# A log-softmax backward kernel: sixteen straight passes become one straight pass and a staged loop

## Chip, cores and metric

One core of a Trainium2 chip. Kernels are compared only within the same rounds. Times are device microseconds (us). "A is x% slower" is computed as the mean time of one kernel's runs over that of the other's of the same rounds, so it is not quite the ratio of the medians that stand beside it.

## The reference

```python
# y, dy: [8, 1024, 8192] float32
softmax_x = np.exp(y)
sum_dy = np.sum(dy, axis=-1, keepdims=True)
out = dy - softmax_x * sum_dy
```

8192 rows of 8192 columns; each tensor is 268.4 MB, so 805.3 MB must move in any case.

## The kernel before

A group is 256 rows (128 partitions, two rows in each, a tile of 8.39 MB), and there are 32. A pass treats two: six tiles in seven transfers (dy, y, dy, y in two halves, two stores), all issued by SP. There is little room: two dy tiles, in which the result is built as well, and one y tile a little longer than a group, in which the second group's y begins to overwrite the first's. So what SP may issue depends on what VectorE has finished and which stores have landed.

```python
    def sums(x):                                   # negated row sums, one row on each engine
        nc.vector.tensor_reduce(out=s_t[:, 0:1], in_=x[:, :D], ..., op=ALU.add, negate=True)
        nc.scalar.activation(x[:, D:], x[:, D:], COPY, accum_out=second_t[:])
        nc.vector.tensor_scalar(out=s_t[:, 1:2], in0=second_t[:], scalar1=-1.0, ...)
    ...
    def compute(x, s_t, at, r, pieces):            # three pieces to a row
        for b, e in pieces:
            nc.scalar.activation(y_t[:, ys], y_t[:, ys], EXP)
            nc.vector.scalar_tensor_tensor(out=x[:, xs], in0=y_t[:, ys], scalar=s_t[:, r : r + 1],
                                           in1=x[:, xs], op0=ALU.mult, op1=ALU.add)

    for g in range(0, G, 2):                       # 16 passes, all unrolled
        load_dy(g, x_ts[0])
        load_y(g, SHIFT, 0, W)
        s_t = sums(x_ts[0])
        for r in range(R):
            compute(x_ts[0], s_t, SHIFT, r, PIECES_A)
        load_dy(g + 1, x_ts[1])
        s_t = sums(x_ts[1])
        for r in range(R):
            load_y(g + 1, 0, r * D, (r + 1) * D)
            compute(x_ts[1], s_t, 0, r, PIECES_B)
        for j in range(2):
            nc.sync.dma_start(out=out_v[g + j], in_=x_ts[j][:])
```

## Time and profile before

| | before |
|---|---|
| time, median (range) of 4 runs | 1866.73 us (1866.56 to 1866.97) |
| span of the profiled run | 1866.1 us |
| VectorE, ScalarE busy | 46%, 37% |
| DMA queue, share of 16 engines' span | 99.8%, 432 GB/s |

The prediction below shows the page, the chain and the timeline.

### The profile page before, as it was taken

Reading aid. Unit: us, or ns where it says so; the run is one execution under the profiler, and the core shown is the slowest. Engines: PE = TensorE matmul, PEld = TensorE weight load, DVE = VectorE, ACT = ScalarE, POOL = GpSimd, SP = SyncE. Lnnn points to the kernel's source line nnn. Section 1 sums busy time; section 2 is a strip of 40 time slices with the busy share of each in tenths; the row PEclk is TensorE's granted clock in tenths of the full one; section 3 lists DMA queues with packets and bytes.
Section 4 is the critical chain, followed back from the end, with each engine's and each line's share of the span. In section 5 each row is a group of like instructions: output and inputs, shape, how many; then the busy total and the mean of one; then the engine's idle time right before and its main releaser. Section 6 shows DMA issues by size and latency. Waiting matters only on the chain.

```text
span 1866.1 us, 843 instructions
## 1 busy us (share of the span) xinstructions
DVE 857.9 (46%) x256; ACT 689.3 (37%) x257; POOL 0.2 (0%) x4
## 2 busy tenths in 40 slices
DVE  2907429074290742807328073280732806338163
ACT  2606326063260532605326053260523605235152
POOL 0000000000000000000000000000000000000000
DMA  9999999999999999999999999999999999999998
GB/s 427 427 427 427 431 444 429 427 434 443 427 434 438 425 435 442 428 429 431 440 431 430 438 427 436 437 440 427 430 438 435 428 437 428 438 435 434 434 428 386
DMA packets 16134, 805.36 MB, mean 432 GB/s; under 512 B 1792, under 2 KB 1792, under 8 KB 1792
## 3 DMA queue, kind: packets, MB, share of 16 engines
q1 hardware_dynamic: 16128, 805.31, 99.8%
q14 instruction: 6, 0.05, 0.0%
HBM read 536.87 MB, written 268.44 MB: 432 GB/s over the span
## 4 chain that ended last, share of the span: by engine, by line
DMA 65%; DVE 14%; another core or an unknown queue 10%; ACT 9%; issue 0%; DVEq 0%; ACTq 0%; SPq 0%
DMA x<-in_dy_dram 31%; DMA out_dram<-x 30%; DVE x L74 14%; ACT x L60 6%; ACT y_t L73 3%; DMA y_t<-in_y_dram 3%; DVEq L121 0%; ACTq L121 0%; SPq L52 0%; ACTq L73 0%; ACTq L60 0%
## 5 line engine op out<-in xcount | busy, mean ns | idle before, releaser
L74 DVE SCALAR_TENSOR_TENSOR x<-y_t,s_t,x 128x1024 f32<-128x1024 f32 (+2 forms) x192 | 579.4, 3059 | 257.5 <-ACT y_t L73 257.5
L57 DVE TENSOR_REDUCE s_t<-x 128x1 f32<-128x8192 f32 x32 | 277.8, 8682 | 721.9 <-DMA x<-in_dy_dram 721.9
L73 ACT ACTIVATE y_t<-y_t 128x1024 f32<-128x1024 f32 (+2 forms) x192 | 460.1, 2466 | 280.0 <-DMA y_t<-in_y_dram 280.0
L60 ACT ACTIVATE x<-x 128x8192 f32<-128x8192 f32 x32 | 225.0, 7030 | 863.2 <-DMA x<-in_dy_dram 863.2
L60 ACT ACTIVATION_READ_ACCUMULATOR x<-x 128x1 f32 x32 | 6.0, 187 | 0.0
L61 DVE TENSOR_SCALAR s_t<-second_t 128x1 f32<-128x1 f32 x32 | 4.6, 143 | 0.0
L60 ACT ACT_TABLE_LOAD x1 | 1.3, 1283 | 0.7 <-PEq L110 0.7
L110 POOL MEMSET const-uint8-127<- 128x1 uint8 x1 | 0.1, 102 | 0.0
L110 POOL MEMSET const-bfloat16-1.0<- 128x1 bf16 x1 | 0.1, 101 | 0.0
L110 POOL MEMSET const-float32-0.0<- 128x1 f32 x1 | 0.1, 98 | 0.2 <-issue 0.2
L110 POOL MEMSET const-float32-1.0<- 128x1 f32 x1 | 0.1, 98 | 0.0
## 6 DMA issues: line engine op xcount, KB each, us to landing
y_t<-in_y_dram SPq DMA_DIRECT2D x32, 4096.0 KB, 22.1
x<-in_dy_dram SPq DMA_DIRECT2D x32, 48.4
out_dram<-x SPq DMA_DIRECT2D x32, 32.6
y_t<-in_y_dram SPq DMA_DIRECT2D x16, 57.5
```

What stands on the lines that cost most here:

```text
L57: nc.vector.tensor_reduce(out=s_t[:, 0:1], in_=x[:, :D], axis=mybir.AxisListType.X, op=ALU.add, negate=True)
L60: nc.scalar.activation(x[:, D:], x[:, D:], COPY, accum_out=second_t[:])
L61: nc.vector.tensor_scalar(out=s_t[:, 1:2], in0=second_t[:], scalar1=-1.0, scalar2=None, op0=ALU.mult)
L73: nc.scalar.activation(y_t[:, ys], y_t[:, ys], EXP)
L74: nc.vector.scalar_tensor_tensor(out=x[:, xs], in0=y_t[:, ys], scalar=s_t[:, r : r + 1], in1=x[:, xs], op0=ALU.mult, op1=ALU.add,)
L110: nc = _bacc.Bacc("TRN2", target_bir_lowering=False, num_devices=1)
```

## The change

The intent is a program a fraction as long that runs as fast. A loop must reset its semaphores in each round. A plain loop does so at a barrier. The staged ("staggered") loop cuts the body into four stages instead: an engine enters a stage only when all five have reported the stage before last as done. The reports default to late points, so the change places some by hand. It also states that the two stores don't depend on each other, since with a row number known only at run time the dependency analysis must assume that they may.

```diff
-    for g in range(0, G, 2):
-        load_dy(g, x_ts[0])
-        load_y(g, SHIFT, 0, W)
+    def done_early():
+        for engine in (mybir.EngineType.Activation, mybir.EngineType.DVE):
+            tc.previous_stage_wait(engine)
+
+    def two_groups(h, boundary, early):
+        load_dy(h, 0)
+        load_y(h, 0, SHIFT, 0, W)
+        boundary()
+        early()
         s_t = sums(x_ts[0])
         for r in range(R):
             compute(x_ts[0], s_t, SHIFT, r, PIECES_A)
-        load_dy(g + 1, x_ts[1])
+        load_dy(h, 1)
+        boundary()
+        early()
         s_t = sums(x_ts[1])
         for r in range(R):
-            load_y(g + 1, 0, r * D, (r + 1) * D)
+            load_y(h, 1, 0, r * D, (r + 1) * D)
             compute(x_ts[1], s_t, 0, r, PIECES_B)
-        for j in range(2):
-            nc.sync.dma_start(out=out_v[g + j], in_=x_ts[j][:])
+        boundary()
+        stores = [nc.sync.dma_start(out=out_v[h, j], in_=x_ts[j][:]) for j in range(2)]
+        tc.declare_no_dep(stores[1].ins, stores[0].ins, reason="different rows of out")
+
+    two_groups(0, lambda: None, lambda: None)
+    with tc.For_i(1, G // 2, 1, iteration_sync="staggered") as h:
+        two_groups(h, tc.stage_boundary, done_early)
```

Cut: the index of the group is split in two (`h`, `j`) in the views and helpers.

## The prediction

> **What bounds the kernel now.** I read the page first. Its opening lines carry the argument: no compute engine is busy for half of the span, and the DMA engines are busy in every slice.
>
> ```profile
> span 1866.1 us, 843 instructions
> DVE 857.9 (46%) x256; ACT 689.3 (37%) x257; POOL 0.2 (0%) x4
> DMA packets 16134, 805.36 MB, mean 432 GB/s; under 512 B 1792, under 2 KB 1792, under 8 KB 1792
> q1 hardware_dynamic: 16128, 805.31, 99.8%
> q14 instruction: 6, 0.05, 0.0%
> ```
>
> 805.31 MB is exactly two inputs and one output of 268.4 MB each, so no byte is moved twice, and the queue's packets fill 99.8% of the engines' time. The kernel can become faster only if the same bytes move at a higher rate, or slower only if the queue runs dry.
>
> Next, the chain that ended last, in order of time (start, length, what). I take it for the rhythm, not for its shares.
>
> ```profile
> 450.09 38.98 DMA x<-in_dy_dram
> 529.22 37.31 DMA out_dram<-x
> 566.55 38.78 DMA x<-in_dy_dram
> ...
> 1613.11 38.60 DMA x<-in_dy_dram
> 1729.17 38.60 DMA x<-in_dy_dram
> ```
>
> One pass over two groups takes 566.55 - 450.09 = 116.46 us, and late in the run 1729.17 - 1613.11 = 116.06. A pass moves six tiles of 8.39 MB; 116.06 / 6 = 19.34 us a tile, 434 GB/s. The best passes have no gap at all.
>
> Third, the timeline of one pass, to see how much work the queue holds whenever the issuing engine, SP, has to issue something (start, length, engine, line, operation).
>
> ```profile
> 489.10 8.69 DVE L57 TENSOR_REDUCE s_t<-x 128x1 f32<-128x8192 f32 x1 [46.92 <-DMA x<-in_dy_dram]
> 508.50 14.32 ACT L73 ACTIVATE y_t<-y_t 128x1024 f32<-128x1024 f32 x6 [12.22 <-DMA y_t<-in_y_dram]
> 512.46 16.73 DVE L74 SCALAR_TENSOR_TENSOR x<-y_t,s_t,x 128x3328 f32<-128x3328 f32 x5 [1.58 <-ACT y_t L73]
> 516.17 9.25 SPq L67 DMA_DIRECT2D y_t<-in_y_dram  x2
> 527.79 7.03 ACT L60 ACTIVATE x<-x 128x8192 f32<-128x8192 f32 x1 [4.96 <-DMA x<-in_dy_dram]
> 529.22 29.78 SPq L95 DMA_DIRECT2D out_dram<-x  x2
> 547.29 7.22 ACT L73 ACTIVATE y_t<-y_t 128x2048 f32<-128x2048 f32 x3 [2.55 <-DMA y_t<-in_y_dram]
> 551.89 6.75 DVE L74 SCALAR_TENSOR_TENSOR x<-y_t,s_t,x 128x3072 f32<-128x3072 f32 x2 [0.30 <-ACT y_t L73]
> 566.55 0.34 SPq L52 DMA_DIRECT2D x<-in_dy_dram  x1
> 566.99 0.77 SPq L67 DMA_DIRECT2D y_t<-in_y_dram  x1
> 585.84 0.33 SPq L52 DMA_DIRECT2D x<-in_dy_dram  x1
> ```
>
> What an engine was released by tells when a transfer landed: dy of the first group at 489.1, its y at 508.5, dy of the second at 527.8, the halves of its y at 537.5 and 547.3, the stores (each releases the load into its own buffer) at 566.5 and 585.8. Against this I set the issue times and get the reserve, the work still queued at an issue:
> - y halves: issued from 516.17; dy of the second group lasts until 527.8. Reserve 11.6 us.
> - first store: issued 529.22; the y halves last until 547.3. Reserve 18.1 us.
> - second store: VectorE ends at 551.89 + 6.75 = 558.64, and the issue follows at once; the first store lasts until 566.5. Reserve 7.9 us, the smallest of the pass.
> - next dy: issued 566.55, when the first store has landed; the second lasts until 585.8. Reserve 19.3 us.
> - second dy: issued 585.84; dy and y lie in the queue, 38.7 us.
> A delay on SP below its reserve costs nothing.
>
> **What the Trainium skill says.** "DMA: Bandwidth & Descriptors", section Specifications, gives a fabric ceiling of 435 GB/s and about 358 GB/s of HBM for one core. The trace agrees with the first (432 over the span, 434 in a clean pass) and not with the second. "Advanced Engine Details and Errata", section Control Flow Timing, puts an unconditional branch at about 51 ns and a compare-and-branch at about 108 ns; before has no loop, so its trace cannot say. "Runtime: NRT & Kernel Launch", section Instruction fetch mechanics, says that a taken branch to a page out of the window stalls for a fetch by DMA; before shows only straight fetching, the 6 packets above. The DMA page's section "Anatomy of one DMA" puts the fixed cost of a transfer near 2.0 us (for the other way of issuing). Here the first load is issued at 0.73 and first used at 22.47: 21.74 less 19.34 of data is 2.4 us. That is what an empty queue would cost each time, and I use 2.4.
>
> **The change part by part.** I compared the built programs engine by engine.
>
> *Removed:* 14 of 16 straight copies of a pass: one stays ahead of the loop, one becomes the body, run 15 times. Transfers, sizes, order and issuing queue stay, as do all compute instructions: 16 x 116.06 = 1857.0 us of data remains. SP's program falls from 98 rows to 28, VectorE's from 226 to 36. So most of the 6 instruction fetches should vanish. The ceiling of what this can give is the excess of the uneven passes: the 14 intervals between successive first loads, from 100.82 to 1729.17, sum to 1628.35 us, against 14 x 116.06 = 1624.84, so 3.5 us in all, of which the fetches are part. I put in -1 us.
>
> *Added, loop entry:* a barrier of all engines, once. VectorE ends the first pass near 92.9 (the first pass matches the one above), SP next needs to issue at 100.82. An estimate of 1 us fits into 7.9. Cost 0.
>
> *Added, stage handshakes:* four stages. Before each, SP counts down "my stage before last is done", waits until all five engines have, resets counters of another stage and reports itself in. That is 2 to 5 semaphore instructions a boundary; no row shows one of these, so I take an estimate of 0.1 us each, guided by the skill's branch figures: 0.2 to 0.5 us. I checked what each boundary waits for:
> - before the first store: all have finished the first group. Here the early report matters. ScalarE and VectorE report it at the start of the second group's work, after their own last piece of the first (VectorE near 529.2), not when the second group is done. The first store moves from 529.2 to at most 529.7, against 18.1 us. Cost 0.
> - before the next dy: the second group is done (558.64) and the back edge is taken. SP has some ten short instructions here, estimated 1.1 us: it is ready near 560, and must wait for the first store until 566.5 anyway. Cost 0.
> - before the second dy: both stores have landed. The load into that buffer waits for the second store anyway, and 38.7 us are queued. Cost 0.
> - before the y halves: the first group's loads have landed (508.5). The free buffer comes later, at 516.2. Cost 0.
> VectorE pays a handshake between its groups, 0.5 us estimated. Its reduction of 8.69 us then ends near 538.3, while the first piece starts at 539.47, since it waits for ScalarE: inside 1.2 us. The 7.9 us reserve at the second store is untouched.
>
> *Added, addresses:* one register instruction for each of 7 transfers, placed before the wait for data or followed by a queue that is full. 0.
>
> *Declared:* the second store need not wait for the first. In before it doesn't either (issue at 558.7, first landing at 566.5), and the built after waits for VectorE alone there. This keeps what was, and gains nothing.
>
> *End:* the barrier after the loop runs under the last store, about 27 us long (558.64 to 585.84 in the middle). Only GpSimd's second reset instruction comes after the landing, estimated at 0.4 us, with nothing to hide it.
>
> Sum: 1866.65 + 0 x 15 - 1.0 + 0.4 = 1866.05, so 1866.0 us.
>
> **The rivals.**
> 1. The stages serialize: the first store waits until the second group is computed. Then it goes out at 558.6 instead of 529.2, the queue is empty from 547.3 on, 11.3 + 2.4 = 13.7 us a pass, x 15 = 206 us, near 2070. For it: stages alone would do this. Against: the reports stand ahead of the second group in the built program.
> 2. The second store waits for the first: issue at 566.5 into an empty queue, 2.4 us x 15 = 36 us, 1903, just under 2%. Against: the declaration, and no such wait in the program.
> 3. Back edges fetch instructions each time. A stall below 7.9 us is hidden on SP, and the others idle for 46.9 us there. What stays is engine time taken by the fetches: five engines, 15 times, 8 KB each (0.05 MB over 6 packets) at 434/16 = 27 GB/s is 75 x 0.3 = 23 us if all hit the slowest DMA engine; 1889. Against: short programs with a prefetch hint. Still the likeliest loss.
> 4. A gain beyond 3.5 us: needs a higher rate than 434 GB/s. Nothing in the change touches it.
>
> **Range and chances.** The three runs of before lie within 0.4 us. The fetch term gives at most -3.5; the end and a part of rival 3 give up to +4. So 1863.5 to 1870.0. Two per cent is 37 us: downwards it lies below the data's own 1857 us, so 0.01; upwards it needs rival 1, or 2 with 3 on top: 0.02. The rest, 0.97, is the same.
>
> **What would show it.** Right: 805.3 MB, 99.8% again, passes of 116.1 us, the first store issued within 0.5 us of VectorE's end, the second about 7.9 us before the first lands, few instruction packets. Wrong: DMA slices below 9 or passes of 118 us and more (rivals 1 and 2), the first store issued near the end of the second group (1), the second at the first's landing (2), dozens of instruction packets (3). A VectorE that starts pieces later than 1.2 us after ScalarE's would show that a handshake is larger than I took it.

## More of the kernel before

One more view is needed to see later where waits have gone: SP's own waits (who waited for whom: us in total, times, longest). The two longest are

```profile
SPq L67 <- DMA y_t<-in_y_dram: 615.0, 16, 39.7
SPq L95 <- DVE x L74: 526.6, 32, 30.0
```

L67 issues the loads of y, L95 the stores. SP waits for most of the run. That is healthy here: it waits with work in the queue behind it.

## The result

After: 1867.24 us median (1867.09 to 1868.33, 4 runs) against 1866.73; ratio 1.0004, 95% interval 0.9987 to 1.0021. The same time, inside the predicted range. All outputs are right.

The page of the changed kernel:

```profile
span 1865.5 us, 2114 instructions
DMA packets 16130, 805.33 MB, mean 432 GB/s; under 512 B 1792, under 2 KB 1792, under 8 KB 1792
q1 hardware_dynamic: 16128, 805.31, 99.9%
q14 instruction: 2, 0.02, 0.0%
```

The executed instructions rise from 843 to 2114 (handshakes and branches on all five engines, address registers on SP), the instruction fetches fall from 6 packets to 2, and the data packets are the same in number and bytes. Of these only the data packets are as unchanged as the time.

The chain in order of time, the first loads of the first and the last pass of the loop:

```profile
101.13 38.63 DMA x<-in_dy_dram
...
1728.62 38.52 DMA x<-in_dy_dram
```

14 passes in 1627.49 us, 116.25 us each. Before, the same 14 took 1628.35 us (100.82 to 1729.17).

The timeline of the same pass as in the prediction:

```profile
512.04 16.73 DVE L75 SCALAR_TENSOR_TENSOR x<-y_t,s_t,x 128x3328 f32<-128x3328 f32 x5 [1.52 <-ACT y_t L74]
528.99 8.69 DVE L58 TENSOR_REDUCE s_t<-x 128x1 f32<-128x8192 f32 x1 [0.22 <-DVE x L75]
529.20 29.43 SPq L105 DMA_DIRECT2D out_dram<-x  x2
...
551.49 6.75 DVE L75 SCALAR_TENSOR_TENSOR x<-y_t,s_t,x 128x3072 f32<-128x3072 f32 x2 [0.32 <-ACT y_t L74]
566.24 0.35 SPq L53 DMA_DIRECT2D x<-in_dy_dram  x1
```

VectorE ends the first group at 512.04 + 16.73 = 528.77. The handshake is the 0.22 us before its reduction, which before started without a gap, and the 0.43 us until SP issues the first store, which before was 0.03 (512.46 + 16.73 = 529.19, issue 529.22). Watch the third row: it runs from the start of the first store's issue to the end of the second's, 29.43 us (29.78 before). It is the yardstick of the experiments.

SP's own waits, the two longest:

```profile
SPq L110 <- DMA y_t<-in_y_dram: 569.3, 15, 38.2
SPq L105 <- DVE x L75: 462.3, 17, 30.1
```

The longest wait has moved from the line of the y load to L110, the loop itself: SP now waits for the same landing at a stage boundary. In length it is the old one (38.2 against 39.7 at most). A handshake wait has taken the place of a data wait that ended at the same moment.

### The profile page after: what moved, and what is told of

It reads as the page before. It is cut to its first block, busy times and chain, and to the rows that moved or that the text cites. A ratio compares the mean times of both kernels' runs of the same rounds, so it can differ in the third digit from the quotient of the medians.

```text
span 1865.5 us, 2114 instructions
## 1 busy us (share of the span) xinstructions
DVE 859.3 (46%) x256; ACT 689.3 (37%) x257; POOL 0.2 (0%) x4
## 3 DMA queue, kind: packets, MB, share of 16 engines
q1 hardware_dynamic: 16128, 805.31, 99.9%
## 4 chain that ended last, share of the span: by engine, by line
DMA 64%; another core or an unknown queue 11%; DVE 11%; ACT 9%; issue 3%; SPq 0%; ACTq 0%; DVEq 0%
DMA x<-in_dy_dram 31%; DMA out_dram<-x 30%; DVE x L75 11%; ACT x L61 6%; DMA y_t<-in_y_dram 3%; ACT y_t L74 3%; SPq L68 0%; ACTq L74 0%; SPq L53 0%; SPq L105 0%; SPq L110 0%; ACTq L110 0%; ACTq L61 0%; DVEq L110 0%
```

## The experiments

Theory: the loop costs nothing because each handshake falls inside a reserve of queued transfers, and the early reports and the declaration are what keep the reserves. Rivals: these hints are decoration; or the loop does cost something each pass that the saved fetches pay back.

### 1. No early reports at all (e1_no_early)

```diff
-        early()          # in both places
```

> Both early reports taken out. My theory (rival 1 of the prediction, now made real): the changed kernel keeps its time only because the two reports stand early. Without them the y halves of the second group are let go only when VectorE has come to the end of the first group's pieces (525 to 529 us on the prediction's clock instead of 516), and the first store only when it has come to the end of the second group's (555 to 559 instead of 529), while the queue is empty from about 547 on. If a report goes out when VectorE's last piece starts: (8.2 + 2.4) x 15 = 159 us, about 2026. If when it ends: 3.8 + 13.7 = 17.5 a pass, 262 us, about 2130. The rival (the reports are decoration, since the queue is full anyway): 1867, within 0.5%.

Measured: 2020.09 us (2 runs) against 1866.9; 8.2% slower. The reports are not decoration.

### 2. Only the second group's report taken out (e1b_first_report_only)

```diff
         load_dy(h, 1)
         boundary()
-        early()
```

> Only the report in the second group is taken out, which lets the first store go; the report that lets the y halves go stays. My theory: the y halves go at 516 as before, the first store at 555.5 (the report goes out when VectorE's last piece starts: 10.6 us a pass, 159 us, about 2026) or at 558.7 (when it ends: 13.7 us, 206 us, about 2073). It is then at least 90% of what both reports are worth if the y halves have reserve enough, and some 80% if not. Rival (decoration): 1867.

Measured: 2020.13 us (2 runs), as slow as without both. This one report, which lets the first store go, is worth it all. The timeline of one of its passes:

```profile
830.09 7.22 ACT L74 ACTIVATE y_t<-y_t 128x2048 f32<-128x2048 f32 x3 [2.55 <-DMA y_t<-in_y_dram]
834.76 6.75 DVE L75 SCALAR_TENSOR_TENSOR x<-y_t,s_t,x 128x3072 f32<-128x3072 f32 x2 [0.32 <-ACT y_t L74]
837.84 4.05 SPq L104 DMA_DIRECT2D out_dram<-x  x2
```

The last half of y landed at 830.09 and emptied the queue. ScalarE's last piece ends at 830.09 + 7.22 = 837.31. The first store is issued 0.53 us later, while VectorE still has a piece to do (until 841.51). So the report left when the *wait* of VectorE's last piece was met and not when the piece was done: the trace has the report itself, a semaphore instruction of VectorE, at 837.45, before that piece starts at 838.09. The queue stood empty for 837.84 - 830.09 = 7.75 us; with 2.4 us for a transfer into an empty queue that is 10.15 us a pass, and the time says 153.2 / 15 = 10.2. The two stores stand 4.05 us apart (start to end) instead of 29.43.

### 3. Only the first group's report taken out (e1c_second_report_only)

```diff
         load_y(h, 0, SHIFT, 0, W)
         boundary()
-        early()
```

> Only the report in the first group's stage is taken out, which lets the y halves of the second group go. The halves had a reserve of 11.6 us. If the report goes out when VectorE's last piece of the first group starts (525.3), the halves are issued at about 525.7, still 2.1 us before the queue is empty at 527.8: no change, 1867 within 0.3%. If it goes out when that piece ends (529.2): 1.4 + 2.4 = 3.8 us a pass, 57 us, about 1924 (ratio 1.03). It tells which of the two figures of the other runs holds, too.

Measured: 1869.22 us median of 4 runs (1868.05 to 1875.41) against 1866.9; ratio 1.002, interval 1.0001 to 1.004.

```profile
755.42 2.17 SPq L68 DMA_DIRECT2D y_t<-in_y_dram  x2
759.95 7.03 ACT L61 ACTIVATE x<-x 128x8192 f32<-128x8192 f32 x1 [4.96 <-DMA x<-in_dy_dram]
```

Both halves of y now go out together, 4.53 us before the transfer ahead of them lands (ScalarE's start at 759.95). They still come in time. The forecast of no change holds, but not by the timing that it gave: it let the report go with the start of VectorE's last piece, which in the trace is 757.15, and the halves go out 1.7 us before that, 0.43 us after ScalarE's last piece ends (754.99), as in experiment 2. What the remaining 2 us are, and the one run at 1875, stays open.

### 4. The stores declared nothing (e2_no_decl)

```diff
-        tc.declare_no_dep(stores[1].ins, stores[0].ins, reason="different rows of out")
```

> The declaration that the second store doesn't depend on the first is taken out; in the loop the second store then waits for the landing of the first. My theory (rival 2 of the prediction): it is issued at 566.5 into an empty queue instead of 558.7, 2.4 us a pass, 36 us, 1903, ratio 1.019. Rival: the 16 DMA engines don't end the first store together, so that part of the 2.4 us is filled or, for those that end early, grows; then anything from 15 to 60 us. If the declaration were idle: 1867.

Measured: 1916.05 us (4 runs) against 1866.9; 2.6% slower, 49.15 / 15 = 3.28 us a pass where I had expected 2.4.

```profile
777.05 38.31 SPq L105 DMA_DIRECT2D out_dram<-x  x2
800.27 6.75 DVE L75 SCALAR_TENSOR_TENSOR x<-y_t,s_t,x 128x3072 f32<-128x3072 f32 x2 [0.32 <-ACT y_t L74]
816.19 0.35 SPq L53 DMA_DIRECT2D x<-in_dy_dram  x1
```

The mechanism is rival 2 of the prediction: VectorE is done at 807.02, the second store goes out some 8 us later, at about 815.0, when the first has landed. The size was off because that landing was: the first store lands 37.83 us after its issue, where in the changed kernel it took 36.90 (the "DMA out_dram<-x" pieces of the two chains), so the second is late by 38.31 - 29.43 = 8.88 us and not by 7.9. By the prediction's own rule that makes 8.88 - 7.9 + 2.4 = 3.4 us a pass. Why the first store lands later was not found out.

### 5. A plain loop with a barrier (e3_barrier_loop)

```diff
-    with tc.For_i(1, G // 2, 1, iteration_sync="staggered") as h:
-        two_groups(h, tc.stage_boundary, done_early)
+    with tc.For_i(1, G // 2, 1) as h:
+        two_groups(h, lambda: None, lambda: None)
```

> The same loop with a plain back edge instead of stages: all transfers must have landed and all engines meet before the next pass. My theory: what the stages are for is the first load of the next pass under the second store. Here that load waits for the second store, the queue runs empty once a pass: 2.4 us for a transfer into an empty queue and 1 to 3 us for the landing's wait, the barrier and the branch: 3.4 to 5.4 us x 15 = 51 to 81 us, 1918 to 1948. A rival that has the back edge free (the queue fills at once): under 20 us.

Measured: 1934.1 us (4 runs) against 1867.05; 3.6% slower, 4.5 us a pass, inside the expected 3.4 to 5.4.

```profile
843.15 0.35 SPq L53 DMA_DIRECT2D x<-in_dy_dram  x1
843.78 0.35 SPq L68 DMA_DIRECT2D y_t<-in_y_dram  x1
844.33 0.33 SPq L53 DMA_DIRECT2D x<-in_dy_dram  x1
```

All three loads of a new pass go out within 1.5 us, since everything has landed. In the staged loop the third follows the first by 19.6 us (585.83 against 566.24), each behind the store it waits for. What the stages buy is the first load under the second store.

### 6. All sixteen passes in the loop (e4_loop_all)

```diff
-    two_groups(0, lambda: None, lambda: None)
-    with tc.For_i(1, G // 2, 1, iteration_sync="staggered") as h:
+    with tc.For_i(0, G // 2, 1, iteration_sync="staggered") as h:
```

> All 16 passes in the loop, no straight pass ahead. My theory: the passes of the loop cost the same as straight ones, so only the loop's entry moves, from under the stores of the first pass to ahead of the first load, where nothing hides it: +0.5 to +2 us, 1868 to 1869 (ratio 1.000 to 1.001). Rival (each pass of the loop pays something that fewer instruction fetches pay back in the changed kernel): the 16th pass adds the same again, which is under 1 us too; the two are told apart by where the first load is issued (0.7 us before).

Measured: 1868.23 us median (4 runs) against 1867.05; ratio 1.0005, interval 0.9988 to 1.0022.

```profile
1.97 0.40 SPq L53 DMA_DIRECT2D x<-in_dy_dram  x1
```

The first load goes out at 1.97 us instead of 0.73. This 1.24 us is the loop's entry, and it is of the size of the whole difference of medians, 1.2 us, though the interval can't show so little. The straight pass ahead of the loop hides the entry under the first pass's stores; the theory's 0.5 to 2 us held.

### 7. to 10. Using up the reserve at the second store

An idle reduction of n columns on VectorE in each second group, in all 16 passes:

```diff
+            if r == 1:
+                extra_t = stats.tile([P, 1], fp32, name="extra_t")
+                nc.vector.tensor_reduce(out=extra_t[:], in_=x_ts[0][:, :n], ..., op=ALU.add)
             compute(x_ts[1], s_t, 0, r, PIECES_B)
```

n = 4096 (e5_dve_4us):

> The changed kernel with one idle reduction of 4096 columns (about 4.3 us) on VectorE in each second group, ahead of the last three pieces. VectorE had 1 us of idle time there, so it ends about 3.6 us later and the second store goes out some 3.6 us later. My theory (reserve of 7.9 us): no change, ratio 1.000 within 0.2%. Rival (the reserve is a mean over 16 DMA engines, and those that end early lose): up to 3.6 x 16 = 58 us.

n = 12288 (e6_dve_13us):

> The same with 12288 columns, about 13 us. VectorE ends about 12.3 us later, the second store goes out 4.4 us after the first has landed, into an empty queue: 4.4 + 2.4 = 6.8 us x 16 = 109 us, about 1976, ratio 1.058. If the reserve were larger than 12.3 us: 1867. If there were none, 12.3 x 16 = 197 us, 2064.

The first two gave 1867.49 us (4 runs; ratio 1.0002) and 1941.62 us (4 runs; 4.0% slower) against 1867.05. The second fell short of its 1976. The trace of n = 12288 shows why:

```profile
788.64 39.62 SPq L110 DMA_DIRECT2D out_dram<-x  x2
797.10 12.95 DVE L105 TENSOR_REDUCE extra_t<-x 128x1 f32<-128x12288 f32 x1
809.96 17.93 DVE L75 SCALAR_TENSOR_TENSOR x<-y_t,s_t,x 128x2048 f32<-128x2048 f32 x6
```

The scheduler had put the reduction ahead of all six pieces, so VectorE's own idle time absorbed more of it than I had assumed: the second store came 39.62 - 29.43 = 10.2 us later and not 12.3. With that lateness the expectation's rule gives 10.2 - 7.9 + 2.4 = 4.7 us a pass, some 1942 us, as measured. The same holds for n = 4096, where only 1.66 us of lateness was left, so that run proves less than was planned. Two more sizes then, with the absorbed 2.6 us in the reckoning.

n = 8192 (e8_dve_9us):

> 8192 idle columns: 8.7 us, of which VectorE absorbs 2.6 in its own waits, so the second store comes about 6.1 us later, 1.9 us ahead of the landing of the first. First packets follow an issue by 1.0 us (first load: issued 0.73, first packet 1.74), so nothing is lost: within 0.2% of 1867. Rival (the reserve of the fastest of the 16 DMA engines counts, it is about 2 us smaller): 5 to 15 us more.

n = 10240 (e9_dve_11us):

> 10240 idle columns: 10.8 us, less 2.6, so the second store comes about 8.2 us later, just after the first has landed. It then pays the empty queue as the kernel without the declaration did (3.28 us a pass): 3.3 to 3.6 us x 16 = 53 to 58 us, 1920 to 1925. If the loss grows smoothly with the lateness rather than from the landing on, it is some 2.2 us a pass: 1900.

They gave 1887.29 us (4 runs; 1.0% slower, where I expected nothing and the rival 5 to 15 us) and 1907.46 us (4 runs; 2.1%, between the two figures expected) against 1867.49. The rows of their second stores, n = 8192 and then n = 10240:

```profile
769.33 35.35 SPq L110 DMA_DIRECT2D out_dram<-x  x2
```

```profile
776.11 37.48 SPq L110 DMA_DIRECT2D out_dram<-x  x2
```

Lateness is the length of that row less 29.43; loss is the median less that of before in the same rounds, over the passes concerned.

| kernel | row, us | lateness | loss a pass | lateness - loss |
|---|---|---|---|---|
| n = 4096 | 31.09 | 1.66 | 0.4 / 16 = 0.0 | |
| n = 8192 | 35.35 | 5.92 | 19.8 / 16 = 1.24 | 4.7 |
| n = 10240 | 37.48 | 8.05 | 40.0 / 16 = 2.50 | 5.55 |
| no declaration | 38.31 | 8.88 | 49.2 / 15 = 3.28 | 5.6 |
| n = 12288 | 39.62 | 10.19 | 74.6 / 16 = 4.66 | 5.5 |

Three kernels that delay the second store in two quite different ways lie on one line: loss = lateness - 5.5. These three can't refute the rule of the expectations ("nothing until the one before has landed, then 2.4 us more"), since past 7.9 us of lateness it is the same line: 7.9 - 2.4 = 5.5. n = 8192 does refute it. Its second store goes out before the first has landed, by some 2 us with the old landing and by 3.4 us with the landing of its own trace, and 1.24 us a pass are lost. So the loss starts ahead of the landing, somewhere between 1.66 and 5.92 us of lateness. n = 8192 also loses 0.8 us more than the line gives; its four runs scatter from 1884.97 to 1889.86.

Two things that no view prints, but the packed traces hold, say more. First, they split the 2.4 us of the first load in part: its first data packet starts 1.0 us after the issue (1.74 against 0.73), and at the end of the run the last landing is recorded 0.44 us after the last data packet ends. So a landing is reported after the data has moved, and the data of a new transfer starts after its issue. The Trainium skill says the like of the landing, for the other way of issuing ("DMA: Bandwidth & Descriptors", section "Anatomy of one DMA": the semaphore update can't fire until the last byte is confirmed landed in the target memory).

Second, each transfer has 16 landings, as many as there are DMA engines, and they don't come together. For n = 8192 those of the first store are spread over 2.3 us in the mean, and the second store goes out 1.1 us ahead of the first of them; in the three kernels on the line they are spread over 0.7 us. If each of the 16 parts needs its next issue 2.4 us ahead of its own landing, an estimate from these landings has the mean part late by 0.9 us for n = 8192, by 2.1, 2.9 and 4.3 us in the three, and by nothing for n = 4096 and in the changed kernel (means of 15 passes of the profiled run). Each is 0.3 to 0.5 us under the loss of its run, n = 8192 too. That favours the rival of the expectations, the reserve counted engine by engine; no run was made to test it. In the changed kernel the second store goes out 5.6 us ahead of the first of the 16 landings in the mean, so by this estimate some 3 us are free for every part.

### 11. and 12. The handshake with the reserve gone (e7_straight_13us, e6_again)

The straight kernel with the same n = 12288, and the loop with it again, 5 rounds side by side.

> The straight kernel of before with the same idle reduction of 12288 columns, to be set against the loop with it (run again beside this one). In the loop's trace that reduction ran ahead of all six pieces of the second group, VectorE had no idle time left from the end of the first group on, and the second store came after its reserve was used up. So what the handshake costs VectorE (0.22 us of idle time between the groups, against none in before) is now on the path. My theory: straight is faster by 0.2 to 0.4 us a pass, 3 to 6 us in all: some 1936 to 1939 against 1941.6 (ratio 0.997 to 0.998 between the two). Rival (the handshake runs beside the data path and costs nothing even there): equal within 1 us. Rival (the back edge, seen here at 0.8 us between second store and next load, counts as well): 12 us or more.

> The same kernel as before with 12288 idle columns in the loop, beside the straight one. It gave 1941.6: again 1941 to 1942.5.

Measured: straight 1937.08 us (1937.01 to 1937.42), loop 1941.46 us (1941.36 to 1941.61), 5 runs each. The loop is 4.38 us slower, ten times the scatter and inside the expected 3 to 6. It doesn't lose all of that in its passes. The last second store of the straight kernel and then of the loop (the ends of the rows):

```profile
1874.27 39.82 SPq L100 DMA_DIRECT2D out_dram<-x  x2
```

```profile
1877.56 39.62 SPq L110 DMA_DIRECT2D out_dram<-x  x2
```

The first pass's second store ends its issue at 102.50 and 102.48, so 15 passes take 1811.59 and 1814.70 us, 120.77 and 120.98 each: 0.21 us a pass, 3.1 us in all. The other 1.3 us come after the last second store. The 0.21 us are in the row of VectorE's reduction at the start of the loop's second group:

```profile
788.52 8.69 DVE L58 TENSOR_REDUCE s_t<-x 128x1 f32<-128x8192 f32 x1 [0.22 <-DVE x L75]
```

The straight one starts its next reduction without that 0.22 us. (The two programs aren't ordered quite alike: the straight one runs the idle reduction ahead of the sums. From the end of the first group to the end of the second VectorE takes 827.96 - 788.30 = 39.66 us in the loop and 826.68 - 787.20 = 39.48 in the straight kernel.) So the handshake is not free: it costs about 0.2 us a pass as soon as VectorE's end sets the second store. In the changed kernel that end comes early enough that nothing is lost. The rival that the back edge counts too (12 us or more) falls. Its length can be read in the first run of n = 12288, where the next load no longer has to wait long for the first store:

```profile
706.92 0.36 SPq L110 DMA_DIRECT2D out_dram<-x  x1
708.11 0.35 SPq L53 DMA_DIRECT2D x<-in_dy_dram  x1
```

At most 708.11 - 707.28 = 0.83 us from the end of the second store's issue to the next load, with the store's 8.39 MB in the queue meanwhile.

## Why the prediction was right, point by point

- **The bound.** Right: the queue is at 99.9%, the bytes are the same, and a pass takes 116.25 us against 116.06 for the best.
- **Stage handshakes, 0 on the path.** Right, and shown from both sides: 0 with the reserve (ratio 1.0004), 0.21 us a pass without. Sizes: 0.5 us was estimated from VectorE's end to the first store, 0.43 measured; up to 0.5 for VectorE between groups, 0.22 measured.
- **The back edge, 0.** Right; estimated at 1.1 us, seen at 0.83 us at most.
- **Loop entry, 0.** Right with the straight pass in front; 1.24 us when it stands at the start.
- **Addresses, 0.** Right in cost. The packed trace has two register instructions ahead of each issue and not one; they take the last 0.15 us before the first store (529.05 to 529.20).
- **The declaration keeps what was.** Right: without it 2.6% slower.
- **Fetches, -1 us.** The packets fell from 6 to 2 and the 14 passes between the first loads took 0.86 us less in the two profiled runs. The timed medians went the other way by 0.5 us, so an effect on the time is not shown.
- **End, +0.4 us.** Not seen in the time: from VectorE's last piece to the end of the span took 28.8 us before (1866.1 - 1837.3) and 28.7 after (1865.5 - 1836.8). It is there in the traces: from the last landing to the end of the span 0.82 us before, 1.45 after, where GpSimd clears semaphores twice instead of once. In the profiled pair the last store landed 0.7 us sooner after its issue, which hid it; that is luck. In experiments 11 and 12 0.81 and 1.45 us stand there, half of the 1.3 us after the last second store.
- **Rival 1, 206 us if made real: measured 153.** The mis-sized term is the time of the report. I had it leave when the second group is done; it leaves when the last piece's wait for ScalarE is met, so the queue stands empty for 7.75 us and not 11.3.
- **Rival 2, 36 us: measured 49.** The mis-sized term is the lateness. The prediction had the second store go out 7.9 us late, at the first's landing; it goes out 8.88 us late, because that landing itself comes 0.93 us later (37.83 against 36.90). In the prediction it put rival 2 at "just under 2%" where 2.6% was measured. The reserve of 7.9 us is too large besides, as n = 8192 shows, but that isn't what this figure missed.
- **Rival 3, fetches at the back edge.** Did not happen: 2 packets in the whole span, against the 75 that it supposed, and both after 1840 us, when no pass was left to issue.

No version tried beats the first one. The 16 passes at 116.06 us are 1857 us of data at 434 GB/s, which leaves 9 us of 1866 for the start, the end and the unevenness, and a staged loop adds nothing that could reach them.

## What to carry to other kernels

For each issue on a saturated queue, list how long the work already queued will last, and subtract the cost of an empty queue (2.4 us here) and, by the estimate above, the spread of a transfer's 16 landings (about 2 us here). A handshake, a branch or an address calculation that fitted into the rest was free here, and from 8 us of lateness on each us counted in full. When a staged loop replaces straight code, look at which *late* report gates an *early* transfer, and at dependencies that only an index unknown until run time creates; here one report was worth 8.2% and one declaration 2.6%, while the loop itself was worth nothing either way. To learn whether a cost is zero or just hidden, use up the reserve on purpose in both versions and compare again.

## What the Trainium skill lacked or had wrong

- "DMA: Bandwidth & Descriptors", Specifications: about 358 GB/s of HBM for one core. The page says further down that this is the share of each when both cores of a pair stream, and that a lone core measured 425. Both kernels here, on a lone core, held 432 GB/s over the whole span, two parts read and one part written, 99% of the page's other limit of 435.
- The same page, "Anatomy of one DMA": the fixed cost of about 2.0 us is a fit for the other way of issuing. For loads issued by SP the first load took 2.4 us beyond its data, and the kernels whose second store came over 7.9 us late fit the same 2.4 us. No page draws the rule that a saturated queue must be refilled ahead of the landing that it waits behind: n = 8192 lost 1.24 us a pass with 3.4 us to go.
- "Advanced Engine Details and Errata", Control Flow Timing: it has branches; the page has elsewhere what it takes to read a semaphore, and another page has the runtime's own barrier around a kernel, but none has the handshake of a loop's stages. Here a stage boundary with its report held VectorE for 0.22 us, delayed a store by 0.4 us, and cost 0.21 us a pass when on the path; a whole back edge on SP, boundary and branch, took 0.83 us at most.
- The same page, Sequencer Loop, says that instructions are pushed into an engine's queue and that others can be read while a control instruction executes, not when a semaphore instruction behind a waiting piece acts. Here the late report was in once the wait of VectorE's last piece was met, 3.7 us before that piece was done (837.84 against 841.51).
